# Gated linear attention scores: two chunks in one product, odd chunks with their rows reversed

## The chip, the cores and the metric

The kernel runs on one core of a Trainium2 chip. Its time is the device time of one execution in microseconds (us). TensorE does the matrix products (rows of the profile call it PE, and its weight loads PEld), VectorE is DVE, ScalarE is ACT, GpSimd is POOL, and SyncE (SP) issues nearly all transfers between HBM and SBUF, the on-chip memory. Products land in PSUM, from where DVE or ACT must fetch them.

## The reference

One layer of a hybrid decoder trunk on 1024 tokens with 16 meta tokens in front and a width of 1024. The mixer projects the normed input, runs a gated linear attention (GLA, 4 heads) and an mLSTM (4 heads) beside each other, gates and merges them; a causal ConvFFN (2816 wide) and two norms follow. Everything is float32. What matters here is the GLA of one head, with key width 128 and value width 256:

```
bc = cumsum(log_a)                        # decay, per key channel
scores[t, s] = sum_k q[t,k] k[s,k] exp(bc[t,k] - bc[s,k])   for s <= t
out = (q * exp(bc)) @ S + scores @ v      # S: state carried from chunk to chunk
```

The decay differs per channel, so scores are no plain product of two matrices. `exp(bc[t] - bc[s])` may be split at a reference row r between s and t, `exp(bc[t] - bc[r]) * exp(bc[r] - bc[s])`, where both exponents are at most zero.

## The kernel before

The kernel works on chunks of 128 tokens, 8 in a head. Within a chunk the triangle of scores is cut into levels of width b = 1, 2, 4, 8, 16, 32 and 64: at level b the chunk falls into blocks of 2b tokens, and a score belongs to the level where s lies in the early half and t in the late half of one block; the reference row is the last of the early half. The diagonal (s = t) has no decay and is a plain product.

For one level, `level(b)` (L610) makes a tile `pk` of 128 channels by 1024 tokens: early tokens hold `k * exp(bc[r] - bc[s])`, late ones `q * exp(bc[t] - bc[r])`. DVE subtracts twice (L624 early, L625 late), ACT takes the exponential (L626), POOL multiplies the early half by k (L627; a plain copy at b = 1, L620) and DVE the late half by q (L628). The decays come from `la` and `bc` (L593 to L606), which hang on a small product `pre` on TensorE (L597). The products then differ by level:

- Levels 1, 2, 4, 8 and 16 (`scores_later`, L580): one product a chunk. The weights are the whole chunk of `pk`, 128 columns, and the moving operand its 64 late columns, so half of the rows that come out are of no use. Eight products a level, into one PSUM bank; DVE then copies the entries that a mask selects into the score tile `A` (L589).
- Levels 32 and 64 (`scores_pair`, L567): `pk` holds all early tokens in its first half and all late ones in its second, so that 128 early columns are of two neighbouring chunks. One product gives both; ACT copies the blocks (L577). Four products a level.
- The diagonal (`scores`, L559) comes first: eight products, and two masked copies on DVE (L565).

`A` holds 8 chunks of 128 by 128, rows s and columns t. At the end `A[:, c, :]` is the weights of the product with v (L720), followed by the state's part (L721).

All those are plain float32 products; the trace shows each as two passes, each with a weight load. The projections around them (`proj_cm`, L154; `proj_v`, L197) take operands split into a high and a low part, in another format (float32r), three passes a block.

What sets the order: each head's GLA is a generator that yields between steps, and `main` (L857) advances it by one step after each third of a projection (24 products, one PSUM tile `pj`, three buffers). Scores of level b/2 follow `level(b)` in a step. A scheduler then places instructions by priority and modelled readiness; every engine runs its queue strictly in the order that results. PSUM tiles of the heads have the tag "s" with three buffers, working tiles of 1040 columns the tag "w" with five.

The masks are built once, early, behind the last of the input's norms (L359 to L373): POOL writes ones (L365) and cuts them by two selections a mask (L367, L369) in a tile `mfs`, DVE casts (L372). `mfs` shares its place (tag "raw") with `raw_s`, into which ACT later writes the small projection (L403) that the decays need.

Of the kernel before, what the change touches and what calls it, by code (L numbers as in the profile page):

```python
# [16 lines left out]
P = 128  # L17
D = 1024
NM = 16
SEQ = 1024  # L20
T = NM + SEQ
# [3 lines left out]
NC = SEQ // P  # L25
H = 4
DV = 256
# [17 lines left out]
def hybrid_kernel(ctx, tc, x, meta, norm_mix, w_in, b_in, gla_w_gate, gla_b_gate, gla_norm,  # L45
                  ml_conv_w, ml_conv_b, ml_norm, w_branch_gla, w_branch_ml, w_out, norm_ffn,
                  ffn_w_up, ffn_conv_w, ffn_conv_b, ffn_w_down, norm_final, out):
    nc = tc.nc
    x, out = x[0], out[0]
# [199 lines left out]
    A = hd.tile([P, NC, P], F32, name="A", tag="A", bufs=1)  # L249
# [107 lines left out]


    with tc.issue_after(last.ins):  # L359
        lmask = {}  # L360
        mfs = hd.tile([P, T], F32, name="mfs", tag="raw", bufs=1)
        for i, b in enumerate((16, 8, 4, 2, 1)):
            mf = mfs[:, 64 * i:64 * (i + 1)]
            half = mf.rearrange("p (n w) -> p n w", w=b)
            nc.gpsimd.memset(half, 1.0)  # L365
            nb = P // (2 * b)
            nc.gpsimd.affine_select(out=half, in_=half, compare_op=OP.is_ge, fill=0.0, base=0,  # L367
                                    pattern=[[-2 * b, nb], [0, b]], channel_multiplier=1)
            nc.gpsimd.affine_select(out=half, in_=half, compare_op=OP.is_ge, fill=0.0, base=b - 1,  # L369
                                    pattern=[[2 * b, nb], [0, b]], channel_multiplier=-1)  # L370
            mu = hd.tile([P, 64], U8, name=f"mu{b}")
            nc.vector.tensor_copy(mu, mf)  # L372
            lmask[b] = mu  # L373
        mu = hd.tile([P, P], U8, name="mu0")
        nc.vector.tensor_copy(mu, ident)
        lmask[0] = mu
        big = hd.tile([P, P], F32, name="big")
# [66 lines left out]
    def wtile(name):  # L444
        return hd.tile([P, T], F32, name=name, tag="w", bufs=5)
# [102 lines left out]
    def state(name):  # L548
        return hd.tile([P, DV + 1], F32, name=name, tag="S", bufs=4)

    def gla(s):
        h = s
        hh = heads[s]
        kT, qT, vt = hh["k"], hh["q"], hh["v"]
        kv, qv = kT[:, NM:T], qT[:, 2:NP]
        def lv(t, b):
            return t.rearrange("p (n h w) -> p n h w", h=2, w=b)

        def scores(lt, rt, b):  # L559
            for g in range(2):  # L560
                pt = ps.tile([P, 4, P], F32, name=f"sc{s}_{b}_{g}", tag="s", bufs=3)
                for i in range(4):
                    c = 4 * g + i
                    nc.tensor.matmul(pt[:, i, :], lt[:, P * c:P * (c + 1)], rt[:, P * c:P * (c + 1)], start=True, stop=True)
                nc.vector.copy_predicated(A[:, 4 * g:4 * g + 4, :], lmask[b][:, None, :].to_broadcast([P, 4, P]), pt)  # L565

        def scores_pair(pk, b):  # L567

            m = 64 // b
            pt = ps.tile([P, 4, P], F32, name=f"sc{s}_{b}", tag="s", bufs=3)  # L570
            for i in range(4):
                nc.tensor.matmul(pt[:, i, :], pk[:, P * i:P * (i + 1)], pk[:, 512 + P * i:512 + P * (i + 1)], start=True, stop=True)
            A2 = A.rearrange("p (i c) t -> p i c t", c=2)
            for c in range(2):
                for n in range(m):
                    p0 = b * (m * c + n)
                    nc.scalar.activation(A2[2 * b * n:2 * b * n + b, :, c, 2 * b * n + b:2 * b * (n + 1)],  # L577
                                         pt[p0:p0 + b, :, p0:p0 + b], AF.Copy)

        def scores_later(pk, b):  # L580

            n = P // (2 * b)
            pt = ps.tile([P, NC, 64], F32, name=f"sc{s}_{b}", tag="s", bufs=3)
            for c in range(NC):
                l = lv(pk[:, P * c:P * (c + 1)], b)[:, :, 1, :]
                nc.tensor.matmul(pt[:, c, :], pk[:, P * c:P * (c + 1)], l, start=True, stop=True)
            dst = A.rearrange("p c (n h w) -> p c n h w", h=2, w=b)[:, :, :, 1, :]
            m = lmask[b].rearrange("p (n w) -> p n w", w=b)[:, None].to_broadcast([P, NC, n, b])
            nc.vector.copy_predicated(dst, m, pt.rearrange("p c (n w) -> p c n w", w=b))  # L589
# [17 lines left out]
        bcv = bc[:, NM:]  # L607
        yield

        def level(b):  # L610
            pk = wtile(f"pk{s}_{b}")
            n = SEQ // (2 * b)
            if b < 32:
                pv = lv(pk[:, :SEQ], b)
                pe, pl = pv[:, :, 0, :], pv[:, :, 1, :]
            else:
                pe, pl = (pk[:, 512 * i:512 * (i + 1)].rearrange("p (n w) -> p n w", w=b) for i in range(2))
            if b == 1:
                nc.scalar.activation(pl, lv(la[:, NM:], 1)[:, :, 1, :], AF.Exp, scale=1.0 / 16)
                nc.gpsimd.tensor_copy(pe, lv(kv, 1)[:, :, 0, :])  # L620
            else:
                b4 = lv(bcv, b)
                ref = b4[:, :, 0, b - 1:b].to_broadcast([P, n, b])
                nc.vector.tensor_tensor(pe, ref, b4[:, :, 0, :], OP.subtract)  # L624
                nc.vector.tensor_tensor(pl, b4[:, :, 1, :], ref, OP.subtract)  # L625
                nc.scalar.activation(pk[:, :SEQ], pk[:, :SEQ], AF.Exp, scale=1.0 / 16)  # L626
                nc.gpsimd.tensor_tensor(pe, pe, lv(kv, b)[:, :, 0, :], OP.mult)  # L627
            nc.vector.tensor_tensor(pl, pl, lv(qv, b)[:, :, 1, :], OP.mult)  # L628
            return pk

        pk = level(1)
        yield
        yield
        for b in (2, 4, 8, 16, 32, 64):
            nk = level(b)
            if b == 64:
                scores_pair(pk, 32)
            else:
                scores_later(pk, b // 2)
            pk = nk  # L640
            yield

# [11 lines left out]
        nc.vector.tensor_tensor(k14[:, :NM - 1], k14[:, :NM - 1], kT[:, :NM - 1], OP.mult)  # L654
        dl = hd.tile([P, NC], F32, name=f"dl{s}", tag="dl", bufs=2)
        nc.scalar.activation(dl, bl.rearrange("p n w -> p (n w)"), AF.Exp, scale=1.0 / 16)
        scores_pair(pk, 64)
        yield

        qh = wtile(f"qh{s}")  # L660
# [37 lines left out]
        op = ps.tile([P, 2, DV], F32, name=f"omp{s}", tag="ot", bufs=2)  # L698
# [5 lines left out]
        def o(c):  # L704
            return oraw[c // 4][:, DV * (c % 4):DV * (c % 4 + 1)]

        for c2 in range(NC // 2):
            op = ps.tile([P, 2, DV], F32, name=f"op{s}_{c2}", tag="ot", bufs=2)
            nup = upd(c2 + 1) if c2 < NC // 2 - 1 else None
            st = []  # L710
            for i in range(2):
                c = 2 * c2 + i
                st.append(S)
                if c < NC - 1:
                    Sn = state(f"S{s}_{c}")
                    nc.vector.scalar_tensor_tensor(Sn[:, :DV], S[:, :DV], dl[:, c:c + 1], up[:, i, :], OP.mult, OP.add)
                    S = Sn
            for i in range(2):
                c = 2 * c2 + i
                nc.tensor.matmul(op[:, i, :], A[:, c, :], vt[:, c + 1, :DV], start=True, stop=False)  # L720
                nc.tensor.matmul(op[:, i, :], qh[:, P * c:P * (c + 1)], st[i][:, :DV], start=False, stop=True)  # L721
# [197 lines left out]
    for j in range(NK):  # L919
# [4 lines left out]
        pt = prod3(ubg[j], og, j < 2, f"bg{j}")  # L924
# [16 lines left out]
    for j in range(NK):  # L941
# [6 lines left out]
        pt = prod3(ubm[j], om_, j < 1, f"bm{j}")  # L948
# [39 lines left out]
    for p in "HL":  # L988
        t = rb.tile([P, 28, W0], F32R, name=f"B{p}0", tag=f"B{p}0")
# [222 lines left out]
    for i, tiles in enumerate(([1, 5, 2, 6, 0], [3, 7, 4, 8])):  # L1212
        for n in range(4):
# [13 lines left out]
            for it, t in enumerate(rest):  # L1227
                pt = po_bank(n, t, ("V1", "X1")[it % 2])
# [19 lines left out]
    for q in range(NJ):  # L1248
        for p in range(2):
            g = piece(q, p)  # L1250
# [185 lines left out]
```

## Time and profile before

| what | value |
|---|---|
| time, median of 3 runs | 1974.15 us (1971.41 to 1975.38) |
| time of the profiled execution | 1973.3 us |
| its span, first to last instruction | 1971.4 us |
| granted TensorE clock, mean | 0.996 |
| busy: PE, DVE, ACT, POOL | 98%, 49%, 38%, 15% of the span |
| projections and heads on TensorE | about 10 to 976 us; the four GLA heads lie between 91 and 526 us |

A group's row in the profile names the line, the engine, the operation, what it writes and reads, the shapes and the count, then its busy time in us and the mean of one in ns, then how long the engine idled just before. A row of the timeline has the start in us from the span's start, the time to the last end of a merged run of equal instructions, engine, line, operation and count. Successive passes on PE overlap, so their price is the distance between starts, not their own duration.

### The profile page before, as it was taken

The page shows a single profiled execution, that of the slowest core. Times are in us where ns is not written, and L with a number is a line of the kernel's source. Part 1 is how long each engine was busy: PE and PEld are TensorE (multiplying, and loading weights), DVE is VectorE, ACT ScalarE, POOL GpSimd, SP SyncE. Part 2 cuts the span into 40 slices and gives each one's busy share as a digit, 9 for nine tenths or more (in the row PEclk, how much of TensorE's full clock was granted, in tenths as well). Part 3 has the DMA queues.
Part 4 walks back from the last instruction along what each step waited for, and adds up shares of the span by engine and source line. Part 5 has one row for each costly group of instructions (what it writes and reads, how often), then busy time and mean ns, then how long its engine had stood idle before and what let it go on. Part 6 is the DMA issues. An engine that isn't in the chain of part 4 may idle for free. (4 is left out here: it accounts for less than half of the span.)

```text
span 1971.4 us, 31346 instructions
## 1 busy us (share of the span) xinstructions
PE 1936.3 (98%) x13333; PEld 1854.0 (94%) x13333; DVE 963.4 (49%) x1427; ACT 744.3 (38%) x1176; POOL 286.5 (15%) x201
## 2 busy tenths in 40 slices
PE   7999999999999999999999999999999999999998
PEld 6999999999999999999999999999999999978886
DVE  6265263637535343422022446698888888710202
ACT  5145333535534343423221234544545444431211
POOL 2020020101000000000000002012222222364220
PEclk9999999999999999999999999999999999999999
DMA  4210403232234222226971433333333333487731
GB/s 152 57 33 23 100 22 95 37 70 69 61 96 90 64 88 63 79 62 123 315 268 54 150 108 108 124 102 126 116 119 123 118 118 113 170 301 263 239 101 43
DMA packets 191271, 224.82 MB, mean 114 GB/s; under 512 B 11102, under 2 KB 150640, under 8 KB 191131
## 3 DMA queue, kind: packets, MB, share of 16 engines
q1 hardware_dynamic: 190843, 221.76, 37.2%
q8 instruction: 105, 1.72, 0.4%
q10 hardware_dynamic: 288, 1.05, 0.1%
q14 instruction: 35, 0.29, 0.0%
HBM read 166.07 MB, written 56.71 MB: 113 GB/s over the span
## 5 line engine op out<-in xcount | busy, mean ns | idle before, releaser
L1323 PE MATMUL pd<-ringH,a 128*128 128x512 f32 x416 | 131.6, 393 | 1.5 <-DMA a<-adrL 1.5
L154 PE MATMUL pj<-xH,wH_r 128*128 128x342 f32 x384 | 124.2, 323 | 0.4 <-ACT r L426 0.4
L154 PE MATMUL pj<-xH,wL_r 128*128 128x342 f32 x384 | 122.9, 320 | 0.0
L154 PE MATMUL pj<-xL,wH_r 128*128 128x342 f32 x384 | 122.5, 319 | 0.0
L1357 DVE TENSOR_TENSOR acc<-pd,acc 128x512 f32<-128x512 f32 x16 | 11.1, 692 | 196.3 <-PE pd L1323 196.3
L1323 PEld LDWEIGHTS pd<-ringH,a 128*128 128x128 f32 x416 | 78.0, 188 | 19.6 <-DMA a<-adrL 2.0
L1323 PE MATMUL pd<-ringL,a 128*128 128x512 f32 x208 | 82.5, 397 | 1.5 <-POOL ringL L1302 1.5
L197 PE MATMUL pv<-wH_gv,xH 128*128 128x256 f32 x256 | 75.4, 294 | 0.0
L197 PE MATMUL pv<-wH_mv,xH 128*128 128x256 f32 x256 | 74.2, 290 | 0.0
L1193 PE MATMUL po<-wL_wo,yH 128*128 128x256 f32 x256 | 72.0, 282 | 2.0 <-DVE wL_wo L103 2.0
L1193 PE MATMUL po<-wH_wo,yH 128*128 128x256 f32 x256 | 72.8, 284 | 0.9 <-DVE h L1200 0.9
L154 PEld LDWEIGHTS pj<-xH,wH_r 128*128 128x128 f32 x384 | 72.2, 188 | 1.1 <-ACT r L426 0.5
L627 POOL TENSOR_TENSOR pk<-pk,kT 128x512 f32<-128x512 f32 x24 | 40.2, 1685 | 226.9 <-ACT pk L626 226.8
L197 PE MATMUL pv<-wL_gv,xH 128*128 128x256 f32 x256 | 72.7, 284 | 0.0
L197 PE MATMUL pv<-wH_gv,xL 128*128 128x256 f32 x256 | 72.6, 283 | 0.0
L154 PEld LDWEIGHTS pj<-xL,wH_r 128*128 128x128 f32 x384 | 72.2, 188 | 0.0
L154 PEld LDWEIGHTS pj<-xH,wL_r 128*128 128x128 f32 x384 | 72.2, 188 | 0.0
L197 PE MATMUL pv<-wL_mv,xH 128*128 128x256 f32 x256 | 71.9, 281 | 0.0
L197 PE MATMUL pv<-wH_mv,xL 128*128 128x256 f32 x256 | 71.9, 281 | 0.0
L1193 PE MATMUL po<-wH_wo,yL 128*128 128x256 f32 x256 | 71.8, 281 | 0.0
L1154 DVE SCALAR_TENSOR_TENSOR cv<-u,fc,cv 128x1024 f32<-128x1024 f32 x44 | 69.4, 1578 | 0.4
L201 DVE TENSOR_TENSOR v<-pv,bB 128x256 f32<-128x256 f32 x64 | 27.0, 421 | 78.1 <-PE pv L197 77.9
(618 smaller groups left out, 6714.5 us busy)
## 6 DMA issues: line engine op xcount, KB each, us to landing
rd<-in_ffn_w_down_dram SPq DMA_DIRECT2D x36, 512.0 KB, 5.9
rg<-in_ffn_w_up_dram SPq DMA_DIRECT2D x22, 512.0 KB, 4.2
ru<-in_ffn_w_up_dram SPq DMA_DIRECT2D x22, 512.0 KB, 3.8
a<-adrH SPq DMA_DIRECT2D x44, 256.0 KB, 5.0
a<-adrL SPq DMA_DIRECT2D x44, 256.0 KB, 4.7
adrH<-aH SPq DMA_DIRECT2D x21, 512.0 KB, 2.6
adrL<-aL SPq DMA_DIRECT2D x21, 512.0 KB, 2.6
wr_r<-in_w_in_dram SPq DMA_DIRECT2D x16, 512.0 KB, 4.0
```

Source lines behind the costliest of these rows:

```text
L154: nc.tensor.matmul(pt[:, :n], a[:, k, :], b[:, k, base + t0:base + t0 + n], start=(i == 0), stop=(i == 3 * NK - 1))
L197: nc.tensor.matmul(pt[:, :DV], a[:, k, t0:t0 + P], b[:, k % 4, :], start=(i == 0), stop=(i == 3 * NK - 1))
L201: nc.vector.tensor_tensor(vt[:n, c, :DV], pt[:n, :DV], bB[:n, :], OP.add)
L627: nc.gpsimd.tensor_tensor(pe, pe, lv(kv, b)[:, :, 0, :], OP.mult)
L1154: nc.vector.scalar_tensor_tensor(y, u[:, j:SEQ + j], fc[:, j, jj:jj + 1], y, OP.mult, OP.add)
L1193: nc.tensor.matmul(pt[:, :DV], a, b[:, k % 4, :], start=(k == 0 and i == 0), stop=(k == NK - 1 and i == len(terms) - 1))
L1323: nc.tensor.matmul(pts[t][n], a[:, c], b[:, 512 * n:512 * n + 512], start=start and i == 0, stop=stop and i == 2)
L1357: nc.vector.tensor_tensor(acc[:, h], pts[t][n], acc[:, h], OP.add)
```

## The change

The five small levels are handled in pairs of chunks too. Of a pair, the even chunk's early tokens stay in place, rows `2bn .. 2bn+b-1`. The odd chunk's early tokens are written in reversed order, token s at row 127 - s. An early token of the odd chunk then falls just into the rows that the even chunk's late tokens leave free, so that 128 weight columns hold the early tokens of two chunks, and 128 moving columns their late tokens. One product gives both chunks' scores, the odd one's with rows reversed. In detail:

- `level(b)` for b below 32 writes the early half in two instructions (even chunks forward, odd chunks through access patterns with negative steps) on DVE and on POOL; the late half is now contiguous.
- `scores_later` becomes `scores_small`: four products of 128 by 128 and one masked copy, over the same number of elements, into `A`. The masks grow from 64 to 128 columns; the odd half is made for reversed rows.
- After level 16, `turn` multiplies the four odd chunks of `A` by a permutation matrix `flip` in one product of 512 columns a head; ACT copies the result to a new tile `An`.
- The diagonal is no longer the first step, since it must write the odd chunks behind the turn: `scores_diagonal` runs with the products of level 32, in the step of `level(64)`. The head so has one step fewer.
- Levels 32 and 64 and the final products read and write `An` for odd chunks. `An` lies in the place of the output tile `oH` (tag "oH").
- The preparation has one wide memset and 22 selections for masks and flip in place of five and ten, and five wider casts and one copy more of DVE.

```diff
     with tc.issue_after(last.ins):
         lmask = {}
         mfs = hd.tile([P, T], F32, name="mfs", tag="raw", bufs=1)
-        for i, b in enumerate((16, 8, 4, 2, 1)):
-            mf = mfs[:, 64 * i:64 * (i + 1)]
-            half = mf.rearrange("p (n w) -> p n w", w=b)
-            nc.gpsimd.memset(half, 1.0)
...
+        nc.gpsimd.memset(mfs[:, :P * 6], 1.0)
+        for sg in (1, -1):
+            nc.gpsimd.affine_select(out=mfs[:, :P], in_=mfs[:, :P], compare_op=OP.is_ge, fill=0.0, base=-sg * (P - 1),
+                                    pattern=[[sg, P]], channel_multiplier=sg)
+        flip = hd.tile([P, P], F32, name="flip")
+        nc.vector.tensor_copy(flip, mfs[:, :P])
...
+        for i, b in enumerate((16, 8, 4, 2, 1)):
+            mf = mfs[:, P * (i + 1):P * (i + 2)]
+            nb = P // (2 * b)
+            for odd in range(2):
+                half = mf[:, 64 * odd:64 * odd + 64].rearrange("p (n w) -> p n w", w=b)
+                for base, sg in (((P - 1) * odd, -1), (b - 1 - (P - 1) * odd, 1)):
+                    nc.gpsimd.affine_select(out=half, in_=half, compare_op=OP.is_ge, fill=0.0, base=base,
+                                            pattern=[[sg * 2 * b, nb], [0, b]],
+                                            channel_multiplier=sg if odd else -sg)
...
+        def scores_diagonal():
+            for g in range(2):
+                pt = ps.tile([P, 4, P], F32, name=f"sc{s}_0_{g}", tag="s", bufs=3)
+                for i in range(4):
+                    c = 2 * i + g
+                    nc.tensor.matmul(pt[:, i, :], kv[:, P * c:P * (c + 1)], qv[:, P * c:P * (c + 1)], start=True, stop=True)
+                nc.vector.copy_predicated(An if g else A.rearrange("p (i c) t -> p i c t", c=2)[:, :, 0, :],
+                                          lmask[0][:, None, :].to_broadcast([P, 4, P]), pt)
+        def turn():
+            pt = ps.tile([P, 4, P], F32, name=f"sct{s}", tag="s", bufs=3)
+            nc.tensor.matmul(pt, flip, A.rearrange("p (i c) t -> p i c t", c=2)[:, :, 1, :], start=True, stop=True)
+            nc.scalar.activation(An, pt, AF.Copy)
...
-            pt = ps.tile([P, NC, 64], F32, name=f"sc{s}_{b}", tag="s", bufs=3)
-            for c in range(NC):
-                l = lv(pk[:, P * c:P * (c + 1)], b)[:, :, 1, :]
-                nc.tensor.matmul(pt[:, c, :], pk[:, P * c:P * (c + 1)], l, start=True, stop=True)
...
+        def scores_small(pk, b):
+            pt = products(pk, b)
+            dst = A.rearrange("p (i c) (n h w) -> p i (c n) h w", c=2, h=2, w=b)[:, :, :, 1, :]
+            m = lmask[b].rearrange("p (n w) -> p n w", w=b)[:, None].to_broadcast([P, 4, P // b, b])
+            nc.vector.copy_predicated(dst, m, pt.rearrange("p i (n w) -> p i n w", w=b))
-        scores(kv, qv, 0)
-        yield
...
         def level(b):
...
             if b < 32:
-                pv = lv(pk[:, :SEQ], b)
-                pe, pl = pv[:, :, 0, :], pv[:, :, 1, :]
+                e = pk[:, :512].rearrange("p (i n h w) -> p i n h w", n=64 // b, h=2, w=b)
+                pe = [e[:, :, :, 0, :], e[:, :, ::-1, 1, ::-1]]
...
-                nc.vector.tensor_tensor(pe, ref, b4[:, :, 0, :], OP.subtract)
+                for e, _, t in early:
+                    nc.vector.tensor_tensor(e, t[..., b - 1:b].to_broadcast(t.shape), t, OP.subtract)
                 nc.vector.tensor_tensor(pl, b4[:, :, 1, :], ref, OP.subtract)
                 nc.scalar.activation(pk[:, :SEQ], pk[:, :SEQ], AF.Exp, scale=1.0 / 16)
-                nc.gpsimd.tensor_tensor(pe, pe, lv(kv, b)[:, :, 0, :], OP.mult)
+                for e, k, _ in early:
+                    nc.gpsimd.tensor_tensor(e, e, k, OP.mult)
...
             if b == 64:
-                scores_pair(pk, 32)
+                scores_diagonal()
+                scores_large(pk, 32)
             else:
-                scores_later(pk, b // 2)
+                scores_small(pk, b // 2)
+                if b == 32:
+                    turn()
...
-                nc.tensor.matmul(op[:, i, :], A[:, c, :], vt[:, c + 1, :DV], start=True, stop=False)
+                nc.tensor.matmul(op[:, i, :], Ac[c], vt[:, c + 1, :DV], start=True, stop=False)
```

`products` is the four products of `scores_pair`, and `scores_large` is `scores_pair` with odd chunks going to `An`; `Ac[c]` is `An[:, c // 2, :]` for odd c and `A[:, c, :]` for even c.

More of the change, by code (lines that the diff above doesn't have):

```diff
@@ L557, in lv, with products @@
             return t.rearrange("p (n h w) -> p n h w", h=2, w=b)
-        def scores(lt, rt, b):
+        An = hd.tile([P, T], F32, name=f"An{s}", tag="oH", bufs=1)[:, :512].rearrange("p (i t) -> p i t", t=P)
+        Ac = [An[:, c // 2, :] if c % 2 else A[:, c, :] for c in range(NC)]
+        def scores_diagonal():
             for g in range(2):
-                pt = ps.tile([P, 4, P], F32, name=f"sc{s}_{b}_{g}", tag="s", bufs=3)
+                pt = ps.tile([P, 4, P], F32, name=f"sc{s}_0_{g}", tag="s", bufs=3)
                 for i in range(4):
[L563 to L569, printed above, removed]
+                    c = 2 * i + g
[6 more added lines that the diff above has]
+            nc.scalar.activation(An, pt, AF.Copy)
+        def products(pk, b):
             pt = ps.tile([P, 4, P], F32, name=f"sc{s}_{b}", tag="s", bufs=3)
@@ L656, in gla @@
         nc.scalar.activation(dl, bl.rearrange("p n w -> p (n w)"), AF.Exp, scale=1.0 / 16)
-        scores_pair(pk, 64)
+        scores_large(pk, 64)
         yield
```

34 lines of the change are left out of this document (17 added, 17 removed).

## The prediction

> **What bounds the kernel now.** I read the page's busy times first, then its slices, then its chain, and then asked for the stretch in which the GLA heads run.
>
> ```profile
> span 1971.4 us, 31346 instructions
> PE 1936.3 (98%) x13333; PEld 1854.0 (94%) x13333; DVE 963.4 (49%) x1427; ACT 744.3 (38%) x1176; POOL 286.5 (15%) x201
> PE   7999999999999999999999999999999999999998
> PEclk9999999999999999999999999999999999999999
> PE 31%; issue 2%; DMA 1%; POOL 1%; DVE 0%; ACT 0%; SPq 0%; POOLq 0%; DVEq 0%; ACTq 0%
> 41.00:540.00 499.00, 495.67 (x3472) 478.25 (x3471) 240.56 (x362) 209.62 (x346) 55.60 (x42) 1.00 0.23 55
> ```
>
> TensorE is busy for 98% of the span, in every slice but the first and last at 90% or more, and the clock is granted in full. In the stretch from 41 to 540 us, in which all four GLA heads lie, PE idles for 3.3 us of 499, while DVE and ACT are not half busy. So this stretch is as long as the passes that PE issues, and work taken from PE comes off the end, as long as nothing else begins to make it wait. What a pass costs is the distance between starts, and that stands in the timeline.
>
> ```profile
> 91.15 1.95 PE L564 MATMUL sc<-qT,kT 128*128 128x128 f32 x16
> 92.85 0.40 PE L154 MATMUL pj<-xH,wH_r 128*128 128x342 f32 x1
> ...
> 110.16 1.90 PE L586 MATMUL sc<-pk 128*128 128x64 f32 x16
> 111.87 0.40 PE L154 MATMUL pj<-xH,wH_r 128*128 128x342 f32 x1
> 112.11 0.32 PE L154 MATMUL pj<-xL,wH_r 128*128 128x342 f32 x1
> ...
> 138.11 1.05 PE L572 MATMUL sc<-pk 128*128 128x128 f32 x8
> 138.92 0.40 PE L154 MATMUL pj<-xH,wH_gq 128*128 128x342 f32 x1
> 139.16 0.32 PE L154 MATMUL pj<-xL,wH_gq 128*128 128x342 f32 x1
> 139.31 0.32 PE L154 MATMUL pj<-xH,wL_gq 128*128 128x342 f32 x1
> L586 PE MATMUL sc<-pk 128*128 128x64 f32 x320 | 37.9, 271 | 0.0
> ```
>
> These rows decide the case. Sixteen passes (eight products, two passes each) of 64 moving columns take 110.16 to 111.87, 1.71 us; sixteen of 128 columns take 91.15 to 92.85, 1.70 us. Below 128 columns the width costs nothing: 0.107 us a pass, whatever is moved. Eight passes with 128 columns, as one level will have, go from 138.11 until the second projection product behind them at 139.16, 1.05 us; by the same measure the old level goes from 110.16 to 112.11, 1.95 us.
>
> **The change part by part.**
>
> *Small levels.* Each of the 20 bursts (320 passes of L586, 16 each: five levels, four heads) falls from 1.95 to 1.05 us: 0.90 us less, 18.0 us in all, on PE, which sets the length here. The operands have the type and shape of L572's, so I see no bound other than the row. The level-32, level-64 and diagonal products keep their count. The diagonal's burst only moves beside that of level 32; its price is by passes, and I put nothing on the move.
>
> *Turn.* One product of 512 columns a head, two passes, which the trace lacks. The nearest are wide float32 products:
>
> ```profile
> 96.82 2.01 PE L597 MATMUL pre<-raw_s,wg 17*128 17x348 f32 x6
> 98.76 0.42 PE L154 MATMUL pj<-xH,wH_r 128*128 128x342 f32 x1
> 99.02 0.32 PE L154 MATMUL pj<-xL,wH_r 128*128 128x342 f32 x1
> 156.81 0.59 PE L720 MATMUL op<-v,A 128*128 128x256 f32 x2
> 157.24 0.59 PE L721 MATMUL op<-S,qh 128*128 128x256 f32 x2
> ```
>
> Two passes of 256 columns take 0.43 us start to start (156.81 to 157.24), so two of 512 take 0.86 us if nothing is lost at the ends: the lower end. The `pre` burst shows the ends: 2.20 us from 96.82 to 99.02 less one projection pitch of 0.16, so 2.04 us for 2080 columns, where 0.84 ns a column would give 1.75. The loss of 0.29 us is the price of changing over, so 1.15 us is the upper end. I take 1.05, nearer to `pre`, since the turn too stands alone between projection products: 4.2 us for four heads (3.4 to 4.6).
>
> *The turn's wait.* PE runs in order, and the turn needs DVE's masked copy of level 16. In the built order the turn stands six projection products behind the last level-16 product in heads 0 and 2, 12 in head 1, 13 in head 3; all that follows on PE waits with it.
>
> ```profile
> 93.13 0.75 DVE L565 COPY_PREDICATED A<-mu,sc 128x512 f32<-128x512 uint8 x1 [0.16 <-PE sc L564]
> 134.70 1.22 DVE L103 TENSOR_TENSOR wL_gv<-wr_gv,wH_gv 128x1024 fp32r<-128x1024 f32 x1
> ```
>
> Such a copy runs 93.13 to 93.88 behind a burst after which PE went on at 92.85: 1.03 us. Six products cover 0.24 + 5 x 0.16 = 1.04 us. So cover and need are even in heads 0 and 2, and the others have 0.9 us to spare. If DVE is still in one of the weight splits (L103, 1.22 us) as the burst ends, each head waits that long. Between 0 and 4.9 us for all; I take 0.6, since in the built order the split stands behind this copy in heads 0 and 2, and in head 3 it hangs on work of the step before. ACT's fetch into `An` has at least eleven projection products and the diagonal's burst, over 3 us, until level 32 needs the buffer.
>
> *Preparation of the levels.* DVE and POOL get one instruction more for levels 1 to 16, over the same elements. That is off PE's path as long as `pk` is ready. Head 1 at level 16, where much has accumulated:
>
> ```profile
> 259.26 1.80 POOL L627 TENSOR_TENSOR pk<-pk,kT 128x512 f32<-128x512 f32 x1 [2.38 <-ACT pk L626]
> 267.56 1.90 PE L586 MATMUL sc<-pk 128*128 128x64 f32 x16
> 126.30 0.16 DVE L654 TENSOR_TENSOR k<-k,kT 128x15 f32<-128x15 f32 x1
> 116.81 1.27 POOL L627 TENSOR_TENSOR pk<-pk,kT 128x512 f32<-128x512 f32 x1 [2.32 <-ACT pk L626]
> L627 POOL TENSOR_TENSOR pk<-pk,kT 128x512 f32<-128x512 f32 x24 | 40.2, 1685 | 226.9 <-ACT pk L626 226.8
> ```
>
> POOL is done at 261.06, 6.5 us ahead of PE. Four shorter bursts ahead of it take 3.6 us of that, which leaves 2.9 us, or 0.72 us that each of the levels 2 to 16 may take longer. A short DVE operation is 0.16 us, so the split costs DVE at most that; POOL's multiplication is anything from 1.27 to 1.8 us, and two halves add a start, some 0.2 us by DVE's row. An odd half's reversed steps are in no row; from below they may cost nothing. I take 0.3 us a level: hidden. DVE's and ACT's further work, 0.7 us for `An` a head, lies on engines that are half idle.
>
> *Masks.* Twenty selections of 64 columns and two of 128 replace ten, and the first write to `raw_s` waits for their casts.
>
> ```profile
> 29.40 0.82 POOL L367 TENSOR_SCALAR_AFFINE_SELECT mfs<-mfs 128x64 f32<-128x64 f32 x3
> 33.18 2.02 POOL L369 TENSOR_SCALAR_AFFINE_SELECT mfs<-mfs 128x64 f32<-128x64 f32 x2
> 37.27 0.49 ACT L403 ACTIVATE raw_s<-pj,bsm 96x272 f32<-96x272 f32 x1
> 42.73 0.28 PE L154 MATMUL pj<-xH,wH_lr 128*128 128x256 f32 x1
> ```
>
> A selection is 0.27 us alone and up to 1.0 us beside DVE. Starting at 29.1 with some 2.5 us for the memsets, flip and `big`, twenty end at 37 us (all fast) or 52 us (all slow); most of them run after DVE's wide operations, so I expect about 39. PE next needs that PSUM buffer at 42.73. So 3 us are to spare, and I put 0.3 us on the later casts ahead of the input's last splits; the bad end is 10 us.
>
> *Sum.* -18.0 + 4.2 + 0.6 + 0.3 = -12.9 us. Against the profiled execution's 1973.3 us that gives 1960.4; the median of the runs lies 0.85 us above that execution, so I forecast 1961.2 us, 0.65% less.
>
> **Rivals.**
>
> *Preparation becomes the bound (slower).* If reversed steps are dear on POOL or DVE, the chain into `pk` overtakes its cover. With e us more a level, heads like head 1 wait 4 x (e - 0.72) us each, 16 x (e - 0.72) in all; at e = 1.53 the gain is gone, and at e = 2 (a reversed half that costs POOL more than the whole of 1.69 us does today) PE waits 20.5 us, and the time is 1981.7. For it speaks that no row has such a step, and that DVE and POOL already get in each other's way:
>
> ```profile
> 110.78 3.71 POOL L627 TENSOR_TENSOR pk<-pk,kT 128x512 f32<-128x512 f32 x2 [50.93 <-ACT pk L626]
> 111.34 2.01 DVE L624 TENSOR_TENSOR pk<-bc 128x512 f32<-128x512 f32 x1
> 114.96 0.68 DVE L625 TENSOR_TENSOR pk<-bc 128x512 f32<-128x512 f32 x1
> ```
>
> A subtraction beside POOL's products took 2.01 us, one after them 0.68. Against it stands that a reversed step adds no element. Above e = 1.53: 7%. A part of it, or late masks, that eats all but 4 us of the gain: 5%.
>
> *Price by columns (slower).* If a product's price went by its moving columns, eight of 64 would cost what four of 128 do, nothing would be saved, and turn, wait and masks would remain: +5.1 us, 1979.3. The two 16-pass rows above speak against it. 2%. [...]
>
> *The turn waits in every head (still faster).* Copy behind a 1.22 us split in all four heads: 4.9 us in place of 0.6, and 1965.5 us. 8%.
>
> **How the numbers follow.** Forecast 78%. Its own bounds: turn 3.4, no wait, no mask cost gives -14.6, 1959.6; turn 4.6, waits 4.9 and 2 us of masks give -6.5, 1967.7. The runs of before spread by 2 us to either side of the middle, so the range is 1957 to 1968; outside it lie the slower rivals, the part-way case and a little of the forecast's own spread. A measurement of this kernel can tell some 0.2%, 4 us, from no change. Faster by more: 78 + 8 = 86%. Within: 5%. Slower: 7 + 2 = 9%.
>
> **What would show it.** Score products of small levels: 160 passes of 128x128 and bursts of about 1.05 us to the second projection product; the turn as two passes of 128x512, about 1.0 us. No idle time of PE ahead of the small levels' products: if there is, released by POOL or DVE, the preparation has become the bound. A gap of up to 0.3 us ahead of the turn in heads 0 and 2. The first `raw_s` write at 39 to 40 us, and the `pj` products about it unbroken; a gap near 43 us would be the masks. From head 5 on the order of TensorE's instructions is the old one, so a difference there would speak against all of this.

## The result and the profile after

The changed kernel takes 1990.26 us (median of 4 runs, 1989.60 to 1991.35) against 1973.01 us of the kernel before (median of 4 as well): a ratio of 1.0092, with a 95% interval of 1.0077 to 1.0107. It is 17 us slower, where 12.9 us less were forecast. The time lies far above the range.

The page of the kernel after: its span, the engines' busy times, and TensorE's busy tenths.

```profile
span 1987.9 us, 31106 instructions
PE 1933.4 (97%) x13181; PEld 1845.0 (93%) x13181; DVE 967.3 (49%) x1444; ACT 745.3 (37%) x1179; POOL 305.5 (15%) x229
PE   7999989998999999999999999999999999999998
```

TensorE issues 152 passes fewer (13181 for 13333), as planned, but two slices of the heads' stretch have lost a tenth. The heads' stretch again, in the table by stretches (length, busy time of PE, PEld, DVE, ACT and POOL, then the granted clock, the share of the DMA engines and GB/s):

```profile
41.00:540.00 499.00, 475.26 (x3221) 452.07 (x3220) 241.46 (x374) 207.10 (x345) 71.13 (x62) 0.97 0.23 53
```

TensorE stands idle for 23.7 us of these 499 (3.3 us before), and the granted clock has fallen from 1.00 to 0.97. The list of TensorE's waits (total, times, longest) puts nearly all of it at one place:

```profile
PE sct L582 <- DVE A L606: 21.0, 4, 7.2
```

The turn (`sct`, L582) waits four times for DVE's masked copy into `A` (L606), 21.0 us together. Head 0 in TensorE's timeline of the kernel after (start, time to the end of the run, in brackets the idle time ahead and what ended it):

```profile
118.37 1.05 PE L589 MATMUL sc<-pk 128*128 128x128 f32 x8
...
119.42 0.32 PE L154 MATMUL pj<-xL,wH_gk 128*128 128x346 f32 x1
...
123.06 1.05 PE L589 MATMUL sc<-pk 128*128 128x128 f32 x8
...
129.54 1.86 PE L582 MATMUL sct<-A,flip 128*128 128x512 f32 x2 [4.47 <-DVE A L606]
131.49 0.49 PE L154 MATMUL pj<-xL,wH_gk 128*128 128x346 f32 x1
131.78 0.49 PE L154 MATMUL pj<-xH,wL_gk 128*128 128x346 f32 x1
...
133.38 0.32 PE L154 MATMUL pj<-xH,wL_gk 128*128 128x346 f32 x1
133.53 0.32 PE L154 MATMUL pj<-xH,wH_gk 128*128 128x346 f32 x1
```

The score burst costs 1.05 us (118.37 to 119.42), as forecast. Behind the wait of 4.47 us it takes 1.95 us from the turn's start to the second projection product (129.54 to 131.49; 1.02 us in the run with a ready input, below), and the projection products follow each other at 0.29 us (131.49 to 131.78) instead of 0.15 (133.38 to 133.53). The other heads wait 7.18, 4.43 and 4.93 us. What the clock did, by stretches:

```profile
129.50:132.00 2.50, 2.46 (x5) 1.43 (x6) 0.00 (x0) 0.56 (x1) 0.00 (x0) 0.56 0.00 0
132.00:134.00 2.00, 2.00 (x10) 2.00 (x10) 0.00 (x0) 0.04 (x1) 0.00 (x0) 0.70 0.00 0
134.00:140.00 6.00, 6.00 (x48) 6.00 (x47) 2.48 (x3) 2.57 (x6) 0.00 (x0) 1.00 0.24 63
269.00:274.00 5.00, 4.73 (x19) 3.70 (x20) 0.88 (x3) 0.60 (x1) 0.00 (x0) 0.59 0.19 58
378.00:384.00 6.00, 6.00 (x24) 4.97 (x24) 0.00 (x0) 0.89 (x2) 0.00 (x0) 0.64 0.01 3
487.00:493.00 6.00, 5.67 (x22) 4.64 (x23) 0.28 (x1) 1.15 (x2) 0.00 (x0) 0.62 0.34 87
```

Behind each of the four waits the granted clock was 0.56 to 0.70 in these stretches, and 1.00 again in head 0 from 134 us on. Length times the missing share, over the five disturbed rows, is 1.1 + 0.6 + 2.05 + 2.2 + 2.3 = 8.2 us.

Why the copy is late stands in DVE's timeline of the kernel after:

```profile
122.79 0.69 DVE L606 COPY_PREDICATED A<-mu,sc 128x512 f32<-128x512 uint8 x1
123.39 1.21 DVE L674 TENSOR_TENSOR kh<-bc 128x1024 f32<-128x1024 f32 x1
...
125.90 1.24 DVE L677 TENSOR_TENSOR kh<-kh,kT 128x1040 f32<-128x1040 f32 x1 [1.22 <-ACT kh L676]
127.06 0.69 DVE L606 COPY_PREDICATED A<-mu,sc 128x512 f32<-128x512 uint8 x1
127.65 1.22 DVE L690 TENSOR_TENSOR qh<-qh,qT 128x1024 f32<-128x1024 f32 x1
128.79 0.69 DVE L606 COPY_PREDICATED A<-mu,sc 128x512 f32<-128x512 uint8 x1
```

The level-16 product ran from 123.06 to 124.1, but its copy (the last row) starts at 128.79. Ahead of it DVE does, one behind the other, the making of k's decayed copy (from 123.39, with a wait of 1.22 us for ACT in it), the copy of level 8 (127.06), and the multiplication of q's decayed copy (127.65). In the kernel before the copy was late as well, there behind the multiplication of q's copy and a weight split (L103); here TensorE's level-16 burst and DVE's queue:

```profile
132.53 1.89 PE L586 MATMUL sc<-pk 128*128 128x64 f32 x16
134.23 0.41 PE L154 MATMUL pj<-xH,wH_gq 128*128 128x342 f32 x1
...
131.80 1.24 DVE L649 TENSOR_TENSOR kh<-kh,kT 128x1040 f32<-128x1040 f32 x1 [1.22 <-ACT kh L648]
132.96 0.70 DVE L589 COPY_PREDICATED A<-mu,sc 128x512 f32<-128x512 uint8 x1
133.56 1.21 DVE L662 TENSOR_TENSOR qh<-qh,qT 128x1024 f32<-128x1024 f32 x1
134.70 1.22 DVE L103 TENSOR_TENSOR wL_gv<-wr_gv,wH_gv 128x1024 fp32r<-128x1024 f32 x1
135.83 0.72 DVE L589 COPY_PREDICATED A<-mu,sc 128x512 f32<-128x512 uint8 x1
```

There the copy started 1.6 us behind the burst's end (134.23), and nobody on TensorE waited for it. With the diagonal's step gone and shorter bursts TensorE now comes to the level-16 product 9.5 us sooner (123.06 for 132.53), but DVE to its copy just 7.0 us sooner (128.79 for 135.83), since k's and q's decayed copies are still to be made ahead of it. The lag has grown to 4.7 us, and TensorE waits for its end. In heads 1 and 3 a weight split of 1.22 us stands ahead of the copy too (at 265.34 and 485.45 us).

### The profile page after: what moved, and what is told of

Its sections match the earlier page's. It is cut to its first block, busy times and chain, and to the rows that moved or that the text cites. A ratio compares the mean times of both kernels' runs of the same rounds, so it can differ in the third digit from the quotient of the medians.

```text
span 1987.9 us, 31106 instructions
## 1 busy us (share of the span) xinstructions
PE 1933.4 (97%) x13181; PEld 1845.0 (93%) x13181; DVE 967.3 (49%) x1444; ACT 745.3 (37%) x1179; POOL 305.5 (15%) x229
## 3 DMA queue, kind: packets, MB, share of 16 engines
q8 instruction: 103, 1.69, 0.4%
q10 hardware_dynamic: 288, 1.05, 0.1%
## 5 line engine op out<-in xcount | busy, mean ns | idle before, releaser
L652 POOL TENSOR_TENSOR pk<-pk,kT 128x256 f32<-128x256 f32 (+1 forms) x40 | 54.3, 1383 | 184.0 <-ACT pk L650 144.9
```

The lines of the kernel that those rows point to most:

```text
L652: nc.gpsimd.tensor_tensor(e, e, k, OP.mult)
```

## The experiments

Theory A: the products save what was forecast, and more than that is lost because the turn waits for a copy that DVE's order makes late, and because TensorE's clock falls behind these waits (0.56 to 0.70 above). Each ratio is to runs of the kernel before that were made together with the kernel's own.

**The turn with an input that is ready.**

```diff
-            nc.tensor.matmul(pt, flip, A.rearrange("p (i c) t -> p i c t", c=2)[:, :, 1, :], start=True, stop=True)
+            nc.tensor.matmul(pt, flip, kv[:, :512].rearrange("p (i t) -> p i t", t=P), start=True, stop=True)
```

> The turn's product reads the first 512 columns of k instead of the odd chunks of A, so that the odd chunks' small-level scores are left out of the result. It is the same permutation product of the same size, at the same place in TensorE's order, but its input was ready long before: the wait is taken away and the price of the turn stays. Theory A (the loss is the wait for VectorE's masked copy, 4.47 + 7.18 + 4.43 + 4.93 = 21.0 us in the changed kernel, and the slow clock behind each wait, some 1.6 to 2 us a head): no wait of TensorE ahead of the turn, the clock stays full behind it, and the time is 1959 to 1964 us. Rival B (a product of 512 columns is slow by itself, at about 2 us a turn, whatever stands ahead of it): the waits go, the turns stay at 1.8 us or more and the products behind them slow, 1967 to 1971 us. Rival C (the preparation of the levels bounds the heads, and a wait that is taken away comes back at the next score product): TensorE waits as long at the products of the levels 32 and 64, and the time stays above 1980 us.

Measured: 1965.44 us, ratio 0.9962 (0.9948 to 0.9977). The turn did not stay at its place in TensorE's order: with nothing to wait for, it was put directly behind the level-16 product, 6 to 13 projection products earlier. Taking the wait away gives back some 25 us, 4 more than the waits themselves, the turn with the product behind it takes 1.02 us and the clock stays at 1.00 behind it: B and C fall. The time ended 1.4 us above A's range, since in head 1 TensorE still waited, now for a PSUM tile that the same copies held, and from 264 to 268 us the granted clock was 0.85 (TensorE's waits of this kernel):

```profile
PE sc L575 <- DVE A L606: 2.8, 2, 1.9
PE sct L582 <- DVE A L606: 1.3, 1, 1.3
```

**The turn one step later.**

```diff
             if b == 64:
+                turn()
                 scores_diagonal()
...
-                if b == 32:
-                    turn()
```

> The turn is issued one step later, at the start of the step of the level-32 scores, with one third of the head's projection (1.4 to 2.8 us of TensorE's work) between the level-16 product and it. Theory A (a wait of TensorE for a copy that comes at a time of its own): each wait shrinks by the work that was put ahead of it, to about 1.7, 5.8, 1.6 and 3.2 us, 12 us together in place of 21.0; where the wait that is left is short the clock stays up. Time 1972 to 1983 us. If only the length of the wait counted and the clock did not, the gain would be just the 8.7 us, 1981.5 us; if the clock recovers in two heads of four, some 4 us more, 1977 us. Rival C (the preparation bounds): the time stays within 2 us of the changed kernel's 1990.3 us.

Measured: 1975.92 us, ratio 1.0016 (1.0007 to 1.0026). The waits were 1.66, 5.76, 1.58 and 3.19 us, as worked out. Stretches of this kernel behind the turns of heads 0, 2, 1 and 3:

```profile
128.70:132.00 3.30, 3.21 (x23) 2.74 (x24) 2.10 (x4) 0.60 (x1) 0.00 (x0) 1.00 0.23 56
371.30:374.70 3.40, 3.33 (x24) 2.85 (x25) 2.19 (x4) 0.60 (x1) 0.10 (x1) 1.00 0.26 61
264.00:268.00 4.00, 3.95 (x12) 2.92 (x13) 0.79 (x3) 0.60 (x1) 0.00 (x0) 0.50 0.17 50
476.00:479.50 3.50, 3.50 (x17) 3.33 (x16) 0.73 (x1) 0.60 (x1) 0.00 (x0) 0.53 0.48 131
```

Here the waits of 1.66 and 1.58 us at the turn left the clock at 1.00, behind those of 5.76 and 3.19 us it was 0.50 and 0.53: the 14 us gained are more than the 8.8 us by which the waits shrank.

**The turn and what follows it two steps later.**

```diff
-                scores_diagonal()
-                scores_large(pk, 32)
+                pk32 = pk
...
-        scores_large(pk, 64)
         yield
+        turn()
...
         yield
+        scores_diagonal()
+        scores_large(pk32, 32)
+        scores_large(pk, 64)
+        yield
```

> The turn is issued at the start of the step that makes q's decayed copy and the transposes of k, and the diagonal and the two large levels, which must come behind it, get a step of their own behind that one; the number of steps stays what it was before the change. Theory A: some 10 us of projections stand between the level-16 product and the turn, more than the longest wait (7.18 us); no wait is left, the clock stays up, and the time is 1957 to 1964 us, below the 1973.0 us of the kernel before. Rival (the scores of the diagonal and the large levels, now late, hold up the head's output products, or the longer life of the level-32 operands holds up the next head's levels): waits of TensorE of several us a head turn up ahead of the output products or of the next level products, and the time is above 1970 us.

Measured: 1970.34 us, ratio 0.9990 (0.9981 to 1.0000): no difference to the kernel before, above A's range, and the rival's by a hair. No turn waited, but other waits came (TensorE's waits of this kernel):

```profile
PE sc L589 <- POOL pk L652: 4.1, 3, 2.7
PE kt L701 <- ACT An L583: 2.4, 1, 2.4
```

So a late turn is no cure by itself: the next head's levels were late, and the transposes waited for ACT's fetch of the turn. The run also gives the turn's price without a wait. In its trace the two passes start at 135.23 and 135.66, 0.43 us apart, and the next work at 136.08: 0.86 us a turn.

**DVE's order.** TensorE's order stays as changed; on DVE two instructions are put behind the copy of level 16 (`cp`).

```diff
-                scores_small(pk, b // 2)
+                cp = scores_small(pk, b // 2)
...
-        nc.vector.tensor_tensor(chunks(kh[:, NM:]), bl.to_broadcast([P, NC, P]), chunks(bcv), OP.subtract)
+        with tc.issue_after(cp.ins):
+            nc.vector.tensor_tensor(chunks(kh[:, NM:]), bl.to_broadcast([P, NC, P]), chunks(bcv), OP.subtract)
...
-        nc.vector.tensor_tensor(qh[:, :SEQ], qh[:, :SEQ], qv, OP.mult)
+        with tc.issue_after(cp.ins):
+            nc.vector.tensor_tensor(qh[:, :SEQ], qh[:, :SEQ], qv, OP.mult)
```

> TensorE's order stays as in the changed kernel. On VectorE alone the subtraction for k's decayed copy (and with it its multiplication) and the multiplication of q's decayed copy are issued behind the masked copy of level 16 instead of ahead of it. Theory A (the copy is late because VectorE's queue is in order and those instructions, 1.21 + 1.22 of waiting + 1.24 + 1.22 = 4.9 us, stand ahead of it): the waits ahead of the turn fall from 4.47, 7.18, 4.43 and 4.93 us to about 0, 2.3, 0 and 0, the clock stays up in three heads or four, and the time is 1960 to 1968 us. Rival D (VectorE is simply too busy, whatever the order): the waits stay above 15 us together, and the time above 1980 us.

Measured: 1964.53 us, ratio 0.9963 (0.9949 to 0.9977), with waits of 0.11, 3.15, 0.32 and 0.81 us. This is the cause, undone alone: the same work on every engine, 26 us less. DVE's order is another, and with it ScalarE's for the exponential of k's copy; TensorE's is the same except that the turn of head 1 stands two products earlier. DVE's timeline of this kernel, where the copies of levels 8 and 16 now run back to back ahead of the wide operations:

```profile
122.18 1.54 DVE L606 COPY_PREDICATED A<-mu,sc 128x512 f32<-128x512 uint8 x2
123.63 1.21 DVE L675 TENSOR_TENSOR kh<-bc 128x1024 f32<-128x1024 f32 x1
124.76 1.21 DVE L692 TENSOR_TENSOR qh<-qh,qT 128x1024 f32<-128x1024 f32 x1
```

**The kernel before, with one product that reads `A` early.**

```diff
+        def probe():
+            pt = ps.tile([P, 4, P], F32, name=f"sct{s}", tag="s", bufs=3)
+            nc.tensor.matmul(pt, ident, A.rearrange("p (i c) t -> p i c t", c=2)[:, :, 1, :], start=True, stop=True)
+            nc.scalar.activation(An, pt, AF.Copy)
...
                 scores_later(pk, b // 2)
+                if b == 32:
+                    probe()
```

> The kernel before, with one product of 512 columns (the identity by the odd chunks of A) and its copy by ScalarE into a scratch tile behind the level-16 scores; the result does not read it. Twelve passes of the projection lie ahead of the probe, so TensorE comes to it at about 136.3, 270.8, 381.1 and 490.3 us of the profile of before, while the masked copies of level 16 ended there at 136.56, 273.02, 384.06 and 492.77 us. Theory A (the copy was late already, and nothing waited for it): waits of about 0.3, 2.2, 3.0 and 2.4 us, 8 us together, with four probes of 0.86 us, and a slow clock behind the longer ones (0 to 5 us): 1983 to 1990 us, that is 11 to 17 us above before. Rival E (the change itself made VectorE late, by the reversed pieces): waits below 2 us together, and the time is before plus the four probes, 1975 to 1978 us.

Measured: 1989.62 us, ratio 1.0087 (1.0072 to 1.0103), 17.4 us more; the waits were 2.59, 3.01 and 2.47 us in heads 1 to 3, and none to speak of in head 0. So the copy was late before the change made anything short, and E falls; what the change added is further lag, 3.1 us in head 0 (1.6 to 4.7). One product of 0.86 us a head, put where it waits, cost the old kernel 17 us. That the change lost as much is chance, since the change also saved 16 to 17 us elsewhere (below). TensorE's waits of this kernel:

```profile
PE sct L595 <- DVE A L589: 8.1, 3, 3.0
```

And the stretch behind the wait of 2.59 us, where the clock is 0.58:

```profile
273.00:276.40 3.40, 3.40 (x17) 3.14 (x16) 0.00 (x0) 0.60 (x1) 0.00 (x0) 0.58 0.00 0
```

**Useless products ahead of the turn, four and seven.** These tell the length of the wait from the clock behind it.

```diff
             pt = ps.tile([P, 4, P], F32, name=f"sct{s}", tag="s", bufs=3)
+            for _ in range(4):
+                nc.tensor.matmul(pt, flip, kv[:, :512].rearrange("p (i t) -> p i t", t=P), start=True, stop=True)
```

> The changed kernel with four more products of 512 columns (the permutation by k, ready long before) into the turn's own PSUM tile ahead of the turn, which overwrites them. At 0.43 us a pass they fill 3.4 us of each wait with work that nobody needs, so the turn can start no sooner, but TensorE does not stand idle for more than 1.0, 3.7, 1.0 and 1.5 us. Theory A (a wait costs its length and, past a certain length, also the clock): the clock stays full in the heads 0, 2 and 3 at least, the turn takes 0.86 us there instead of 1.9, the products behind it keep their pitch, and the time falls by 1.5 to 2 us a head, to 1982 to 1986 us, although work was added. Rival F (the slow passes behind the wait belong to the turn, not to the idle time): turn and pitches as slow as before, 1990 us or more.

Measured: 1991.44 us, ratio 1.0098 (1.0084 to 1.0111). The forecast for it missed. The scheduler put fillers and turn directly behind the level-16 product, ahead of the projection products that had covered a part; the waits left were 1.98, 4.23, 1.96 and 3.57 us instead of 1.0, 3.7, 1.0 and 1.5, and only head 0 kept its clock. Heads 0 and 2 of this kernel, with waits of 1.98 us (126.76 to 128.74) and 1.96 us (374.47 to 376.43); the last section says why the stretches are cut so:

```profile
124.39:127.81 3.42, 2.37 (x6) 0.76 (x4) 2.71 (x3) 2.51 (x4) 0.00 (x0) 1.00 0.29 87
127.81:131.22 3.41, 2.48 (x12) 2.00 (x13) 0.87 (x2) 0.60 (x1) 0.00 (x0) 1.00 0.00 0
373.57:376.98 3.41, 1.45 (x5) 0.38 (x4) 2.80 (x4) 1.00 (x2) 0.00 (x0) 1.00 0.38 113
376.98:380.39 3.41, 3.41 (x12) 2.89 (x11) 0.00 (x0) 0.60 (x1) 0.00 (x0) 0.50 0.00 0
```

Since this run could not tell A from F, seven fillers followed.

> Seven products of 512 columns that nobody needs ahead of each turn in place of four, 2.57 us more of them a head. The four left waits of 1.98, 4.23, 1.96 and 3.57 us, and the clock fell behind the last three. Theory A: the waits shrink to 0, 1.7, 0 and 1.0 us, so that filler and wait together take 26.7 us of TensorE instead of 25.4, but no wait is long enough to cost the clock, which gives back some 1.5 us in each of three heads: 1991.4 + 1.3 - 4.6 = about 1988 us, faster than with four and faster than the changed kernel without any filler (1990.3 us), although 24 us of useless products are added. Rival F (the slow passes do not come from the idle time): 1992.7 us or more.

Measured: 1986.16 us, ratio 1.0070 (1.0058 to 1.0082). The longest wait at a turn was 1.66 us, and the heads' stretch has its clock again:

```profile
41.00:540.00 499.00, 492.88 (x3290) 459.07 (x3289) 242.46 (x375) 209.02 (x346) 71.05 (x62) 1.00 0.22 53
```

With 24 us of useless products added, the kernel is 4 us faster than the changed one (hardly more than the noise of the two ratios) and 5 us faster than with four fillers. F, which asked for 1992.7 us or more, falls: the turns are all there, and with the long waits the slow passes are gone.

**No turn, and no turn with DVE's order.**

```diff
-            nc.tensor.matmul(pt, flip, A.rearrange("p (i c) t -> p i c t", c=2)[:, :, 1, :], start=True, stop=True)
-            nc.scalar.activation(An, pt, AF.Copy)
+            nc.scalar.activation(An, A.rearrange("p (i c) t -> p i c t", c=2)[:, :, 1, :], AF.Copy)
```

> The changed kernel without the turn's product: ScalarE copies the odd chunks of A into their tile as they stand, so that the odd chunks' small-level scores stay in reversed row order and are wrong in the result. TensorE has neither the turn nor its wait; the products of two chunks, the reversed halves, the masks and VectorE's copies all stay. Theory A (the products of two chunks are worth what the prediction put on them, 20 bursts at 0.90 us = 18.0 us, and all that was lost was lost at the turn): 1972.2 - 18.0 = 1954 us, and up to 4 us more for the waits that VectorE's lag left in head 1 in the run with the ready input: 1953 to 1959 us. Rival H (part of the 18 us is lost elsewhere, in the preparation or by score products that cost more than the burst shows): 1960 us or more, with waits of TensorE ahead of the small levels' products.

Measured: 1963.22 us, ratio 0.9964 (0.9951 to 0.9978). That is H's number, and A as it stood missed: without a turn, other products of TensorE waited for the same copies, which hold PSUM tiles (who waited for the masked copies of this kernel, in us and times):

```profile
  ACT An L581: 8.1, 4
...
  PE sc L575: 2.8, 1
  PE sc L587: 1.5, 1
```

Whether these waits too came from DVE's order was asked next; this kernel has both edits, the one above and that of DVE's order.

> No turn (ScalarE copies the odd chunks as they stand, so their small-level scores are left in reversed row order), and on VectorE k's and q's decayed copies behind the masked copy of level 16. Without the turn alone the time was 1963.2 us, because TensorE waited 2.80 us in head 1 and 1.50 us in head 3 for the PSUM tile that a late masked copy still held. Theory A' (those waits have the same cause as the turn's: the order on VectorE): they go, and what is left is the change's saving on the score products, 17 to 18 us: 1953.5 to 1957 us, some 4 to 7 us below the version with the turn one step later and the same order (1961.1 us), which is the turn's price of four times 0.86 us with its last wait. Rival H (part of the saving is lost elsewhere): 1960 us or more.

Measured: 1956.25 us, ratio 0.9917 (0.9904 to 0.9931), 16.1 us below before; the spans differ by 17.0 us (1954.4 against 1971.4). The waits for the copies of the small levels are gone, and H with them: the score products do save 16 to 17 us.

**DVE's order in the kernel before.** The same two lines behind `cp = scores_later(...)`.

> The kernel before with VectorE's order alone changed in the same way: k's and q's decayed copies behind the masked copy of level 16. Theory A: nothing on TensorE waited for the late copy in the kernel before (3.3 us of idle time in the stretch of the heads), so there is nothing to gain: within 2 us of 1972 us. Rival I (the order on VectorE is a gain by itself, and the 11 us of the best version are partly that and not the change): 1968 us or less.

Measured: 1971.54 us, ratio 0.9997 (0.9989 to 1.0006). The order is worth nothing where nobody waits; rival I falls.

**Both edits together: DVE's order and the turn one step later.**

> VectorE's order with k's and q's decayed copies behind the masked copy of level 16, and the turn one projection third later: both earlier edits together. Theory A: the waits left by the first (0.11, 3.15, 0.32 and 0.81 us) shrink to 0, 1.8, 0 and 0 us; a wait of 1.6 us left the clock full, so head 1 gets its clock back as well (some 2 us). Together 4 to 5 us below the 1964.5 us of the first edit alone: 1959 to 1962 us. Rival G (in head 1 VectorE lags so far that the scores wait for a free PSUM tile wherever the turn stands, 4.1 us in the run with the ready input): about 1963 to 1965 us, no better than the first edit alone.

Measured: 1961.06 us (1959.31 to 1961.30), ratio 0.9942 (0.9930 to 0.9955). Rival G falls. This version beats both kernels, by 11 and by 29 us. Its heads' stretch:

```profile
41.00:540.00 499.00, 494.87 (x3411) 474.16 (x3410) 251.51 (x388) 216.43 (x357) 71.31 (x62) 1.00 0.26 62
```

The clock is 1.00, and the one wait left at the turn is 1.5 us, in head 1:

```profile
PE sct L582 <- DVE A L606: 1.5, 1, 1.5
```

## Why the prediction was wrong

- *Small levels, -18.0 us: right, 6 to 12% high.* That the width costs nothing was seen at two widths alone, 64 and 128 moving columns (1.71 and 1.70 us a burst). Bursts of 1.05 us as forecast; with nothing waiting, 16.1 us by the times and 17.0 by the spans.
- *Turn, +4.2 us: right, a little high.* 0.86 us each without a wait, 3.4 us, its lower end. Both versions with DVE's order, with and without the turn, differ by 4.8 us, and that holds a wait of 1.5 us.
- *The turn's wait, +0.6 us (0 to 4.9): the step that failed.* It counted one product's cover against one copy, with one instruction of DVE ahead at worst. The copy stood behind a list, and the list was in the trace of before: the copy of level 16 started at 135.83 for a burst that ended at 134.23, right behind the split that the prediction shows at 134.70. The forecast also moved TensorE forward by the gain without asking whether DVE moved too. It moved less (7.0 us against 9.5 in head 0), and the waits were 21.0 us. The one row of a copy on which the bound rested (93.13) was of the head's beginning, where DVE's queue was short.
- *Missing altogether: the clock.* It was read as 1.00 and taken as given. The 1.00 of the heads' stretch is rounded: the trace of before has the clock at half for 3.41 us behind a wait of 1.55 us (182.22 to 183.77, for DVE's `or`). TensorE was busy for 1.86 of the 3.41 us ahead of it:

```profile
182.15:185.56 3.41, 1.86 (x13) 1.42 (x13) 2.22 (x10) 0.81 (x1) 1.17 (x1) 1.00 0.00 0
185.56:188.97 3.41, 3.41 (x19) 3.41 (x17) 3.28 (x7) 1.06 (x1) 0.00 (x0) 0.50 0.02 5
```

Added up for the heads of the changed kernel, -17.0 for the products, +20.4 of idle time (23.74 - 3.33), +3.4 for the turns and +8.2 of slow clock make +15.0 us; a product behind the last head (`ga`, 626.96 before) starts at 641.56, 14.6 us later. Most of the rest of the 16.5 us between the spans is the clock again: at 1300.56 us it halves for 3.41 us behind a wait of 2.2 us that both kernels have and that left it whole in the profile of before, and there the distance to the kernel before grows from 14.8 to 16.3 us. TensorE's order is the old one by then, so this difference is no effect of the new score products.
- *Preparation of the levels, nothing: right.* In the group's row of the changed kernel all score products of the levels together waited 0.7 us for POOL and DVE. A reversed step shows no price of its own: in head 3 POOL's forward and reversed halves of level 16 took 1.18 and 1.19 us (at 470.23 and 471.37), DVE's of level 2 0.42 us each (459.60 and 459.93). Two such halves on POOL are some 2.4 us, where the whole took 1.69 on average: 0.7 us more a level and not the 0.3 of the forecast, and still hidden. The group's row:

```profile
L589 PE MATMUL sc<-pk 128*128 128x128 f32 x224 | 29.9, 276 | 0.7 <-POOL pk L652 0.4 <-DVE pk L653 0.3
```

- *Masks, +0.3 us: right as far as it shows.* The first write to `raw_s` came at 39.44 us (forecast 39 to 40), with no gap of TensorE near 43 us; 0.3 us by itself is too small to be measured here. ACT's timeline of the changed kernel:

```profile
39.44 0.48 ACT L410 ACTIVATE raw_s<-pj,bsm 96x272 f32<-96x272 f32 x1 [2.26 <-DVE mu L382]
```

- *The rivals.* "The turn waits in every head" had the mechanism and named one instruction of 1.22 us as its size; 4.4 to 7.2 us a head, with the clock, put it on the slower side, where none of the 9% stood for it. Neither slower rival happened.

The best version, 11 us below before, comes near to the forecast's 12.9: the sum held for a kernel in which the turn hardly waits, not for the one that was to be judged. That its 1961.1 us all but equals the forecast's 1961.2 is luck, since the forecast started from 1974.15 us and the runs of before beside it have a median of 1972.2.

## What to carry to other kernels

Before a product is put behind another engine's result, look up in the trace when that result is ready today, with everything queued ahead of it, and compare it with the time at which TensorE will come, its own gain subtracted. A result that nobody waits for can be late without a trace of it in the waits, as the copy of level 16 was in the kernel before, 1.6 us behind its burst. Where a wait is left, price it with the clock: behind the 1.96 us of idle TensorE in head 2 with four fillers the clock was 0.50 for 3.41 us, by an estimate from these two numbers another 1.7 us lost, and the average clock of 1.00 over 499 us of the kernel before did not rule out the like (3.41 us at 0.50 from 185.56). The cure may lie in the order of the engine that is waited for: here DVE's order took 26 us off the changed kernel, with the same work on every engine.

## What was unexpected of the hardware

An otherwise dense TensorE lost its clock behind a single wait (4.47 us in head 0 of the changed kernel, then 0.50 from 129.79 to 133.20 us). The wait's length alone does not decide: at the turns, 1.58 and 1.66 us left the clock at 1.00, and 2.59 us (the probe), 3.15 us (DVE's order), 3.19 and 5.76 us (one step later) and 4.43 to 7.18 us (the changed kernel) were followed by 0.50 to 0.64, but 1.98 and 1.96 us with four fillers went one way and the other (1.00 and 0.50). Away from the turns, 2.38 us in the kernel with the late turn (head 3, ahead of the transposes) left it whole (1.00 from 488.4 to 497 us), 1.55 us in the kernel before (at 182.22) was followed by 0.50, and 2.21 us in the same profile (up to 1285.88 us) by 1.00.

The profiles show what else counts, where the wait lies. In the profiles of the kernels before and after, between 30 and 1945 us, all times at which the granted clock changes lie whole multiples of 3.413 us apart: in the changed kernel it falls at 129.79, 266.32, 375.55 and 484.77 us, and the distances are 40, 32 and 32 times that. A half clock lasts one or two such stretches (3.41 us in head 0; 6.83 in heads 1 to 3, where it begins during the wait). Cut at multiples of 3.413 us from these times, the two profiles have 5 stretches at full clock in which TensorE was busy for less than 40%, and each was followed by a half clock; of 5 between 50% and 55%, two were; of 1100 above that, none. This fits the two nearly equal waits with four fillers, whose rows above are cut in the same way: in head 0 the wait lies across two stretches, 69% and 73% busy (2.37 and 2.48 us), in head 2 within one, 42% busy (1.45 us). These are counts of a few executions, and the busy time goes by the modelled ends of the passes, so the shares are no limits. What sets the times of the changes is not shown.
